# A Silu in a gated delta rule, queued on ScalarE behind the latest exponential of the keys' norms

## The chip, the cores and the metric

The kernel runs on one core of a Trainium2 chip. The metric is the device time of one execution, in microseconds (us); the runs shown are three, with their median and their ends. The profile is of one further execution, and its times count from the first profiled instruction. Engines are named as the profile names them: PE is TensorE's matmuls, PEld its weight loads, ACT is ScalarE, DVE is VectorE, POOL is GpSimd, SP issues the weight transfers.

## The reference

Two layers over x of shape 1 x 256 x 2048 in float32. Layer 0 is differential attention and a gated MLP with a short convolution. Layer 1 is the gated delta rule, which the change touches, and again the MLP:

```
def gated_deltanet(h, w_in, conv_w, a_log, dt_bias, norm_g, w_out):
    proj = h @ w_in
    ...
    qkv = jax.nn.silu(causal_dwconv(qkv, conv_w))
    q, k, v = jnp.split(qkv, [GDN_KEY_DIM, 2 * GDN_KEY_DIM], axis=-1)
    q = l2_norm(q.reshape(b_sz, s_len, GDN_QK_HEADS, GDN_HEAD_DIM).astype(jnp.float32))
    k = l2_norm(k.reshape(b_sz, s_len, GDN_QK_HEADS, GDN_HEAD_DIM).astype(jnp.float32))
    ...
    o = gated_delta_rule(q, k, v, g, beta)
    o = rms_norm(o, norm_g) * jax.nn.silu(z.reshape(b_sz, s_len, GDN_V_HEADS, GDN_HEAD_DIM).astype(jnp.float32))
    return o.reshape(b_sz, s_len, GDN_VALUE_DIM).astype(h.dtype) @ w_out

def l2_norm(x):
    return x * lax.rsqrt(jnp.sum(x * x, axis=-1, keepdims=True) + RMS_EPS)
```

There are 16 query and key heads of 128 and 32 value heads. So between the projection and the delta rule stand a four-tap convolution, a Silu, and for queries and keys a division by the root of a sum of squares. Inside the delta rule, decays are exponentials of differences of accumulated gates.

## The kernel before

**Dense products.** `dense` (L132) multiplies a weight block of 2048 x 256 by the 256 tokens. It goes through the 2048 rows in four chunks of four 128-row tiles. For each chunk `weights` (L81) transfers a 512 KB tile `raw` on the SP queue (L86), rounds it on ACT to the tile `whi` (the cast on L89) and takes the remainder on DVE as `wlo` (L90). PE then multiplies with both parts (L151, L152, and L154 where the product isn't `wide`). `raw`, `whi` and `wlo` have four buffers each. After every chunk `dense` calls `tick` (L71), which advances each background generator by one `yield`.

**The delta rule.** `gdn` (L542) works in four blocks of four head pairs. In each block the plan is: `("k", 0)` to `("k", 3)`, then `("v", 0)`, two z products, `("v", 1)` to `("v", 3)`, and the output product of the block before. For each `k` and `v` step, `lin` (L576) runs one dense product and scales it, and `convs` (L589) applies the four taps (`conv`, L301: one ACT instruction on L306 and three on DVE, L310, for each half) and then one Silu over 128 x 512 elements on ACT (L593). That is 32 Silus of this kind.

**A key pair's norms.** After each `k` step a generator `keys` (L596) is spawned. At its first advance it squares the Silu's output on ACT (L599) and splits the square into a high part (ACT, L321) and a low part (DVE, L322); `lows` keeps the latter. It then lets three advances pass. At the fourth, which is the last chunk of the next dense product, it emits the sums of squares on PE (L329, two matmuls over the two parts), the addition of the mask on DVE (L626), and then, under `lnexp` (L295), a load of ACT's table set that holds Ln and Exp (L297), the root as Ln (L316) and Exp (L317), and four exponentials of the decays (L631). `lnexp` puts these only behind its own table load, by `issue_after`. DVE then divides by the root (L632), and two advances later PE multiplies the normalised keys and queries (L639, L640) and DVE scales the products (L645, L647). In block 0 the first pair's generator waits until `lows` has two entries, so the roots of the first two pairs are both emitted in the third dense product.

**The order on an engine.** The kernel is built by a framework that keeps one queue for each engine and chooses the order in each queue at build time, from a simulated timeline and the order in which the program emits the instructions (`schedule_with_timeline_sim=True`). An instruction that isn't ready in that simulation can be overtaken by one emitted later. `with tc.issue_after(i)` adds an edge for the ordering alone: what the block emits on the engine of `i` is queued behind `i`. On the chip each engine works through its queue in order and waits by semaphores only for what it needs of other engines.

**Table sets.** Silu isn't in the set with Ln and Exp. Where an activation finds the other set active, the build puts an ACT_TABLE_LOAD in front of it, which the profile shows under the line of that activation: L593 for a Silu of `convs`, L317 and L631 for exponentials, L854 for the Silu of z. The loads on L297 are written in the program and are always there.

Of the kernel before, what the change touches and what calls it, by code (L numbers as in the profile page):

```python
# [10 lines left out]
AF = mybir.ActivationFunctionType  # L11
# [15 lines left out]
class Trunk:  # L27
# [37 lines left out]
    def mp(self):  # L65
        return self.mps.tile([P, 512], F32, tag="mp", name="mp")
# [246 lines left out]
    def rsqrt(self, out, ps, n):  # L313

        nc = self.nc
        nc.scalar.activation(out, ps, AF.Ln, bias=self.eps, scale=1.0 / n)  # L316
        nc.scalar.activation(out, out, AF.Exp, scale=-0.5)  # L317

    def split(self, out, a):

# [221 lines left out]
    def gdn(self, w_gate, w_in, w_z, w_out, nb, hb, gate_ap, const_ap, conv_col, ng, done):  # L542
# [7 lines left out]
        nc, tc, mp = self.nc, self.tc, self.mp  # L550
# [4 lines left out]
        with tc.tile_pool(name="gd", bufs=1) as gd:  # L555
# [15 lines left out]
            flat = "p i c -> p (i c)"  # L571
            nl = 4 * hb
            half = gd.tile([P, 2], F32, tag="half", name="half")
            gates, lows = {}, []

            def lin(w, wide):  # L576
                ps = self.dense(w, KD, self.h_acts, wide=wide)
                u = gd.tile([P, 2, T], F32, tag="u", name="u", bufs=1)
                if wide:
                    main, small = self.halves(ps)  # L580
                    uv = u.rearrange("p c (q j) -> p c q j", q=2)
                    nc.scalar.copy(uv, small)
                    nc.vector.tensor_tensor(uv, main, uv, ALU.add)
                    self.scale(u)
                else:
                    self.merge(ps, u)
                return u

            def convs(u, tiles):  # L589
                c = gd.tile([P, 2, T], F32, tag="cv", name="cv", bufs=4)  # L590
                for i in range(2):
                    self.conv(c[:, i, :], u[:, i, :], [conv_col(t, tiles[i]) for t in range(4)], None)
                nc.scalar.activation(c, c, AF.Silu)  # L593
                return c

            def keys(hq, c, cc, b0, res):  # L596

                sq = gd.tile([P, 2, T], F32, tag="qs", name="qs", bufs=2)
                nc.scalar.square(sq, c)  # L599
                sp = gd.tile([P, 2, 2, T], F32R, tag="qp", name="qp", bufs=1)  # L600
                lows.append(self.split(sp, sq))

                def fetch():
                    d = gd.tile([P, 2, 384], F32, tag="lt", name="lt", bufs=hb)
                    nc.sync.dma_start(d, gates["rows"][2 * hq:2 * hq + 2, :].unsqueeze(0).to_broadcast([P, 2, 384]))
                    return d

                d = fetch() if "rows" in gates else None
                for _ in range(3):
                    yield  # L610
                while "rows" not in gates:
                    yield
                if d is None:
                    d = fetch()
                    yield
                    yield
                    yield
                gc = gates["col"]
                dv = d[:, :, :T].rearrange("p v (t c) -> p v t c", t=2)
                m4 = mask.unsqueeze(1).unsqueeze(1).to_broadcast([P, 2, 2, P])  # L620
                pn = mp()
                sums = self.total(pn, [sp])
                while len(lows) < 2:
                    yield
                with tc.issue_after(lows[max(hq, 1)].ins):
                    nc.vector.tensor_tensor(dv, dv, m4, ALU.add)  # L626
                with self.lnexp(sums):
                    self.rsqrt(sq, self.apart(pn), 1)
                    for v in range(2):
                        for t, s in ((1, d[:, v, :P]), (0, d[:, v, P:])):  # L630
                            nc.scalar.activation(s, s, AF.Exp, bias=gc[:, t, 2 * hq + v:2 * hq + v + 1])  # L631
                nc.vector.tensor_tensor(c, c, sq, ALU.mult)  # L632
                q, k = c[:, 0, :], c[:, 1, :]
                yield
                yield
                prods = []
                for r in (k, q):
                    p = mp()
                    nc.tensor.matmul(p[:, :P], k[:, P:], r[:, P:], start=True, stop=True)  # L639
                    nc.tensor.matmul(p[:, P:384], k[:, :P], r, start=True, stop=True)  # L640
                    prods.append(p)
                lt = d
                qkt = gd.tile([P, 2, 384], F32, tag="qkt", name="qkt", bufs=hb)
                for v in range(2):
                    nc.vector.scalar_tensor_tensor(  # L645
                        qkt[:, v], prods[1][:, :384], P ** -0.5, d[:, v], ALU.mult, ALU.mult)
                    nc.vector.tensor_tensor(lt[:, v], prods[0][:, :384], d[:, v], ALU.mult)  # L647
                for v in range(2):
                    b = b0 + v
                    lv = lt[:, v, :T].rearrange("p (t c) -> p t c", t=2)  # L650
                    for r in quad:
                        nc.gpsimd.tensor_copy(
                            cc[r, :, 2 * b:2 * b + 2].rearrange("p c t -> p t c"), lv[r, :, r])
                    res.append((lt[:, v], qkt[:, v]))
# [180 lines left out]
            for b in range(nb):  # L835
# [5 lines left out]
                for op, i in plan + [("v", i) for i in range(1, hb)]:  # L841
                    if op == "k":
                        hq = heads[i]
                        c = convs(lin(w_in[hq * 2], 0 < b < nb - 1), (hq, nq + hq))
                        self.spawn(keys(hq, c, cc, 2 * i, lqs))
                        if i == hb - 1:
                            self.spawn(invert(b, cc, lqs, inv))
                            self.spawn(levels(lqs, inv, range(len(groups)), solved))
                    elif op == "z":
                        gr = groups[i]  # L850
                        zt = zts[i] = gd.tile([P, 2, gv, P], F32, tag="vz", name="zt", bufs=4)
                        ps = self.dense_tok(w_z[heads[gr[0]] // 2], KD, self.h_acts)
                        for t in range(2):
                            nc.scalar.activation(zt[:, t].rearrange(flat), ps[:, t, :], AF.Silu,  # L854
                                                 scale=self.rstdc[:, t:t + 1])
                    else:
                        gi = i // gh
                        gr = groups[gi]
                        if i == gr[0]:
                            vt = gd.tile([P, 2, gv, P], F32, tag="vz", name="vt", bufs=4)  # L860
                            ready = []
                            self.spawn(group(gi, gr, lqs, solved, vt, ready, zts, acts))
                        hq = heads[i]
                        c = convs(lin(w_in[hq * 2 + 1], True),
                                  (2 * nq + 2 * hq, 2 * nq + 2 * hq + 1))
                        self.spawn(to_tokens(c, vt, 2 * (i - gr[0]), ready))
# [216 lines left out]
```

## Time and profile before

| what | value |
|---|---|
| median of three runs | 2531.76 us (2530.8 to 2531.91) |
| profiled execution, span | 2530.1 us |
| median less span | 1.66 us |
| ACT busy | 1513.2 us, 60% of the span |
| DVE busy | 1908.3 us, 75% |
| ACT_TABLE_LOADs on L297 / L593 | 28 / 18 |
| key stages of blocks 0 to 3, about | 1095 to 1145, 1236 to 1300, 1434 to 1500, 1627 to 1690 us |

The span is from the first to the last profiled instruction, so what is measured outside it (1.66 us) is start and end. Busy shares are of the whole span. In the timeline each row has the start in us, the length in us, the engine, the line, the operation, the tiles it writes and reads, their shapes, and a count where equal neighbours are merged; a bracket at the end tells how long the engine was idle before it and what ended that. PE's rows have modelled ends, so its starts are what to compare.

### The profile page before, as it was taken

To read this page: it belongs to the slowest core of one execution; us is meant where nothing else is said; L and a number is where in the kernel's file an instruction comes from. 1 tells how busy PE (TensorE), PEld (TensorE's weight loads), DVE (VectorE), ACT (ScalarE), POOL (GpSimd) and SP (SyncE) were. 2 spreads that over 40 slices of the span, in tenths; PEclk is the share of its full clock that TensorE was granted. 3 is DMA by queue.
4 is the path that set the end of the run, shared out by engine and by line. 5 is a ranking of instruction groups with operands and counts; after the bars stand their busy time and mean duration, and the time that the engine had idled before them with its cause. 6 is when DMAs were issued, how large, how long until landed. Compare 5 with 4: busy or idle time off the path is not lost.

```text
span 2530.1 us, 41598 instructions
## 1 busy us (share of the span) xinstructions
PE 2520.0 (100%) x16151; PEld 2309.7 (91%) x16151; DVE 1908.3 (75%) x2847; ACT 1513.2 (60%) x2098; POOL 103.5 (4%) x197
## 2 busy tenths in 40 slices
PE   9999999999999999999999999999999999999999
PEld 8998899999999999998989989989999999999998
DVE  8886677777777555689788788788887777776544
ACT  7766656666666444485774675675566666665343
POOL 0000000000000000012021021021000000000000
PEclk9999999999999999999999999999999999999999
DMA  7555566666666666666455565555566666666775
GB/s 256 175 184 175 167 203 201 202 202 201 200 201 202 200 200 202 202 187 201 154 185 180 170 188 184 168 175 184 165 201 201 201 201 202 201 201 205 209 207 157
DMA packets 138199, 487.20 MB, mean 193 GB/s; under 512 B 15472, under 2 KB 18448, under 8 KB 138000
## 3 DMA queue, kind: packets, MB, share of 16 engines
q1 hardware_dynamic: 137712, 484.17, 60.8%
q8 instruction: 127, 2.08, 0.3%
q14 instruction: 72, 0.59, 0.1%
q10 hardware_dynamic: 288, 0.35, 0.0%
HBM read 482.32 MB, written 2.15 MB: 191 GB/s over the span
## 4 chain that ended last, share of the span: by engine, by line
PE 95%; ACT 3%; DVE 1%; issue 1%; DMA 0%; SPq 0%; ACTq 0%; DVEq 0%
PE ps L151 51%; PE ps L152 26%; PE ps L221 3%; PE ps L220 3%; PE ps L222 3%; PE mp L773 2%; PE mp L151 1%; PE ps L154 1%; ACT whi L89 1%; PE mp L329 1%; PE mp L152 0%; ACT L593 0%; ACT lt L631 0%; PE ps L123 0%; ACT L297 0%
## 5 line engine op out<-in xcount | busy, mean ns | idle before, releaser
L90 DVE TENSOR_TENSOR wlo<-raw,whi 128x1024 fp32r<-128x1024 f32 (+2 forms) x911 | 1104.1, 1213 | 506.1 <-ACT whi L89 498.2
L89 ACT CAST whi<-raw 128x1024 fp32r<-128x1024 f32 (+2 forms) x911 | 944.2, 1038 | 822.9 <-PE ps L151 657.0
L151 PE MATMUL ps<-h,whi 128*128 128x512 f32 (+1 forms) x4208 | 1369.4, 375 | 0.0
L152 PE MATMUL ps<-h,wlo 128*128 128x256 f32 x4208 | 1151.1, 274 | 1.0 <-DVE wlo L90 1.0
L151 PEld LDWEIGHTS ps<-h,whi 128*128 128x128 f32 x4208 | 796.1, 189 | 102.8
L152 PEld LDWEIGHTS ps<-h,wlo 128*128 128x128 f32 x4208 | 807.7, 192 | 2.8 <-DVE wlo L90 1.3
L151 PE MATMUL ps<-ac,whi 128*128 128x512 f32 x1546 | 506.8, 382 | 0.0
L152 PE MATMUL ps<-ac,wlo 128*128 128x256 f32 x1546 | 421.2, 273 | 0.0
L151 PEld LDWEIGHTS ps<-ac,whi 128*128 128x128 f32 x1546 | 292.1, 189 | 40.8 <-PE ps L151 0.2
L152 PEld LDWEIGHTS ps<-ac,wlo 128*128 128x128 f32 x1546 | 296.8, 192 | 0.1
L151 PE MATMUL ps<-oc,whi 128*128 128x512 f32 x512 | 170.7, 384 | 0.0
L220 PE MATMUL ps<-whi,h 128*128 128x512 f32 x384 | 146.5, 382 | 0.0
L221 PE MATMUL ps<-wlo,h 128*128 128x512 f32 x384 | 146.1, 380 | 0.0
L222 PE MATMUL ps<-whi,h 128*128 128x512 f32 x384 | 145.7, 379 | 0.0
L310 DVE SCALAR_TENSOR_TENSOR cv<-u,fcols,cv 128x255 f32<-128x255 f32 (+1 forms) x344 | 142.9, 477 | 0.0
L152 PE MATMUL ps<-oc,wlo 128*128 128x256 f32 x512 | 142.0, 277 | 0.0
L151 PEld LDWEIGHTS ps<-oc,whi 128*128 128x128 f32 x512 | 96.9, 189 | 12.5
L152 PEld LDWEIGHTS ps<-oc,wlo 128*128 128x128 f32 x512 | 98.3, 192 | 0.5
L308 ACT ACTIVATE cv<-u,fcols 128x256 f32<-128x256 f32 x172 | 93.9, 593 | 0.5 <-DVE u L205 0.5
L343 DVE TENSOR_TENSOR x<-ps,x 128x512 f32<-128x512 f32 x110 | 75.6, 687 | 12.5 <-PE ps L152 11.2
L310 DVE SCALAR_TENSOR_TENSOR cv<-u,cols,cv 128x255 f32<-128x255 f32 (+2 forms) x192 | 84.0, 486 | 0.3
L221 PEld LDWEIGHTS ps<-wlo,h 128*128 128x128 f32 x384 | 72.6, 189 | 10.0 <-DVE wlo L90 0.2
(220 smaller groups left out, 2077.3 us busy)
## 6 DMA issues: line engine op xcount, KB each, us to landing
raw<-w_up SPq DMA_DIRECT2D x344, 512.0 KB, 4.7
raw<-w_down SPq DMA_DIRECT2D x160, 512.0 KB, 3.8
raw<-w_in SPq DMA_DIRECT2D x128, 512.0 KB, 4.7
raw<-w_z SPq DMA_DIRECT2D x64, 512.0 KB, 3.7
raw<-w_out SPq DMA_DIRECT2D x64, 512.0 KB, 4.2
raw<-w_qk SPq DMA_DIRECT2D x56, 512.0 KB, 4.5
raw<-w_v SPq DMA_DIRECT2D x32, 512.0 KB, 3.5
raw<-w_o SPq DMA_DIRECT2D x32, 512.0 KB, 4.7
```

Of the source, the lines that this page charges most:

```text
L89: self.cast = nc.scalar.copy(hi[:, :, s], raw[:, :, s])
L90: nc.vector.tensor_tensor(lo[:, :, s], raw[:, :, s], hi[:, :, s].bitcast(F32), ALU.subtract)
L151: nc.tensor.matmul(bank[c][:, :n], hi[:, k, s], self.turns(a[:, :n // T, :]), start=first, stop=False)
L152: nc.tensor.matmul(bank[c][:, :T], lo[:, k, s], self.turns(a[:, :1, :]), start=False, stop=last and wide)
L154: nc.tensor.matmul(bank[c][:, :T], hi[:, k, s], self.turns(a[:, 1:, :]), start=False, stop=last)
L220: nc.tensor.matmul(ps[:, c, :], ah, wh, start=first, stop=False)
L221: nc.tensor.matmul(ps[:, c, :], ah, wl, start=False, stop=False)
L222: nc.tensor.matmul(ps[:, c, :], al, wh, start=False, stop=last)
L308: nc.scalar.activation(out, u, AF.Identity, bias=bias, scale=taps[n - 1])
L310: nc.vector.scalar_tensor_tensor(out[:, j:], u[:, :T - j], taps[n - 1 - j], out[:, j:], ALU.mult, ALU.add)
L343: self.nc.vector.tensor_tensor(x, part, x, ALU.add)
L773: nc.tensor.matmul(p[:, v, :], l(v), r[:, v, :], start=i == 0, stop=i == len(terms) - 1)
```

## The change

`rsqrt` (L313) now returns its exponential. `keys` appends that instruction to a list `roots`. In `convs`, if the list has an entry, the Silu is emitted inside `issue_after` of the latest one. The edge is on ACT alone and adds no semaphore. `rsqrt`'s other callers ignore the value. Of the 32 Silus, the first two of block 0 are emitted while the list is empty.

```
@@ rsqrt
         nc.scalar.activation(out, ps, AF.Ln, bias=self.eps, scale=1.0 / n)
-        nc.scalar.activation(out, out, AF.Exp, scale=-0.5)
+        return nc.scalar.activation(out, out, AF.Exp, scale=-0.5)
@@ gdn
-            gates, lows = {}, []
+            gates, lows, roots = {}, [], []
@@ convs
-                nc.scalar.activation(c, c, AF.Silu)
+                if roots:
+                    with tc.issue_after(roots[-1].ins):
+                        nc.scalar.activation(c, c, AF.Silu)
+                else:
+                    nc.scalar.activation(c, c, AF.Silu)
                 return c
@@ keys
                 with self.lnexp(sums):
-                    self.rsqrt(sq, self.apart(pn), 1)
+                    roots.append(self.rsqrt(sq, self.apart(pn), 1))
```

## The prediction

> **What bounds the kernel now.** I read the page first, then busy time by window over the four key stages of the delta rule, then the timeline of ACT, DVE and PE in the stretches where PE stands idle.
>
> ```profile
> span 2530.1 us, 41598 instructions
> PE 2520.0 (100%) x16151; PEld 2309.7 (91%) x16151; DVE 1908.3 (75%) x2847; ACT 1513.2 (60%) x2098; POOL 103.5 (4%) x197
> ```
>
> PE is busy 2520.0 of 2530.1 us. The change adds and removes no matmul, so all that it can give through PE's visible idle time is some of 10.1 us in the whole kernel. The windows tell how much of that lies in the key stages. Their columns are the length, then busy time with counts for PE, PEld, DVE, ACT and POOL, then clock, DMA share and GB/s.
>
> ```profile
> 1095.00:1145.00 50.00, 49.05 (x297) 44.70 (x296) 40.52 (x62) 44.12 (x66) 13.85 (x26) 1.00 0.62 193
> 1236.00:1300.00 64.00, 62.09 (x361) 56.00 (x360) 54.98 (x93) 58.96 (x86) 13.97 (x24) 1.00 0.50 153
> 1434.00:1500.00 66.00, 65.51 (x362) 58.84 (x362) 55.37 (x82) 58.97 (x85) 14.29 (x28) 1.00 0.58 177
> 1627.00:1690.00 63.00, 62.73 (x426) 58.02 (x426) 49.80 (x75) 53.85 (x77) 11.14 (x24) 1.00 0.53 160
> ```
>
> One row is one block. PE is idle 0.95 us in block 0 (50.00 less 49.05), 1.91 in block 1, 0.49 in block 2 and 0.27 in block 3: 3.62 us in all. ACT is busy 88%, 92%, 89% and 85% of them, far over its 60% of the span. Here, and only here, ACT is near enough to being the bound that its order can reach PE.
>
> **Which Silus move.** A pair's root is emitted in the last chunk of the next dense product, just ahead of that product's own Silu; in block 0 two roots come in the third product. So the edge names, for the Silus of pairs 1, 2, 3 and of the first values in each block (in block 0 from pair 2 on), an exponential that is only just emitted; for every other Silu it names one long done, and binds nothing. Where the queue already has that exponential first, nothing changes. Where it is overtaken, the exponential finds the Silu's table set active and needs a load of its own, so the overtakings can be counted in table loads. The first row below is of the view by source line (shortest, median and longest in ns, first and last start); the others are groups of ACT by line.
>
> ```profile
> L317 ACT ACT_TABLE_LOAD  x4: 1283/1283/1283, 1124.2 to 1491.1; - x4
> ```
>
> ```profile
> L631 ACT ACT_TABLE_LOAD x1 | 1.3, 1283 | 0.0
> L854 ACT ACT_TABLE_LOAD x1 | 1.3, 1283 | 0.0
> ```
>
> The four on L317 belong, in the timeline of ACT, to block 0 pair 3, block 1 pairs 1 and 2, and the first values of block 2. The one on L631 belongs to block 0 pair 2, and the one on L854 follows the overtaking in block 2, where the late exponential left the wrong set for z's Silu. So five Silus move, in blocks 0, 1 and 2, and none in block 3. With the exponential first, each place needs one load for its Silu and none to come back, since the load on L297 is written in the program anyway. Six loads of 1.283 us fall away: 7.70 us of ACT, 1513.2 to 1505.5. The loads on L593 and L297 stay at 18 and 28.
>
> **Block 1**, the largest term. ACT, then DVE, then PE:
>
> ```profile
> 1263.07 1.48 ACT L631 ACTIVATE lt<-lt,gc 128x128 f32<-128x128 f32 x4
> 1264.57 1.28 ACT L593 ACT_TABLE_LOAD   x1
> 1265.86 0.63 ACT L593 ACTIVATE cv<-cv 128x512 f32<-128x512 f32 x1
> ...
> 1267.44 1.28 ACT L317 ACT_TABLE_LOAD   x1
> 1268.74 0.63 ACT L317 ACTIVATE qs<-qs 128x512 f32<-128x512 f32 x1
> ```
>
> ```profile
> 1269.40 0.69 DVE L632 TENSOR_TENSOR cv<-cv,qs 128x512 f32<-128x512 f32 x1 [0.71 <-ACT qs L317]
> ```
>
> ```profile
> 1270.14 0.49 PE L639 MATMUL mp<-cv 128*128 128x128 f32 x2 [1.41 <-DVE cv L632]
> ...
> 1273.97 0.45 PE L329 MATMUL mp<-qp,onesr 128*128 128x512 f32 x1 [0.50 <-ACT whi L89]
> ```
>
> The exponential at 1268.74 stands behind a load, the Silu and a second load (3.19 us) and one cast. DVE's division waits for it, and PE's product of keys waits 1.41 us for DVE. With the order turned, both loads and the Silu leave from in front: the exponential starts at 1268.74 - 3.19 = 1265.55, the division ends 3.19 us sooner, and PE, which would have started at 1270.14 - 1.41 = 1268.73, finds it done at 1266.90. So the 1.41 us go. What is late next is the wait of 0.50 us at the sums: its input is ACT work queued behind this place, which comes 1.28 us sooner (one load less), against a PE that comes 1.41 us sooner. It stays at about 0.5. The nearest row of the order to come, and of what then is left, is block 2, whose second pair has its exponential first already:
>
> ```profile
> 1461.09 0.64 ACT L317 ACTIVATE qs<-qs 128x512 f32<-128x512 f32 x1
> ...
> 1463.98 0.63 ACT L593 ACTIVATE cv<-cv 128x512 f32<-128x512 f32 x1
> ```
>
> ```profile
> 1467.12 0.48 PE L329 MATMUL mp<-qp,onesr 128*128 128x512 f32 x1 [0.49 <-ACT qp L321]
> ```
>
> There PE waits 0.49 us at the sums and nowhere else in the stage. I take block 1's idle time to fall from 1.91 to between 0.27 and 0.50: a gain of 1.4 to 1.6.
>
> **Block 0.** ACT, then DVE, then PE:
>
> ```profile
> 1102.61 0.63 ACT L593 ACTIVATE cv<-cv 128x512 f32<-128x512 f32 x1
> ...
> 1104.08 0.63 ACT L599 ACTIVATE qs<-cv 128x512 f32<-128x512 f32 x1
> 1104.73 1.28 ACT L631 ACT_TABLE_LOAD   x1
> 1106.03 1.49 ACT L631 ACTIVATE lt<-lt,gc 128x128 f32<-128x128 f32 x4
> ...
> 1110.80 0.61 ACT L321 CAST qp<-qs 128x512 fp32r<-128x512 f32 x1
> 1111.31 1.05 ACT L89 CAST whi<-raw 128x1024 fp32r<-128x1024 f32 x1
> 1112.26 0.63 ACT L317 ACTIVATE qs<-qs 128x512 f32<-128x512 f32 x1
> ```
>
> ```profile
> 1104.65 0.69 DVE L626 TENSOR_TENSOR lt<-lt,con 128x512 f32<-128x512 f32 x1 [2.02 <-DMA lt<-grow]
> ...
> 1111.45 0.69 DVE L322 TENSOR_TENSOR qp<-qs,qp 128x512 fp32r<-128x512 f32 x1 [1.56 <-ACT qp L321]
> ```
>
> ```profile
> 1113.93 0.38 PE L152 MATMUL ps<-h,wlo 128*128 128x256 f32 x1 [0.95 <-DVE wlo L90]
> ...
> 1117.12 0.57 PE L329 MATMUL mp<-qp,onesr 128*128 128x512 f32 x1
> ```
>
> Pair 2's Silu at 1102.61 must now stand behind the exponential at 1112.26. With it go its square and its cast of `qp`. The four decay exponentials at 1106.03 need the masked rows of DVE, ready at 1104.65 + 0.69 = 1105.34, so of what leaves from in front of them they gain only 0.69 us. The cast of `qp` at 1110.80 (0.61) goes too, so the weight cast at 1111.31 comes 0.69 + 0.61 = 1.3 us sooner, and DVE no longer waits 1.56 us for `qp` ahead of the remainder that PE lacks at 1113.93. That covers the 0.95 us. I book 0.7 to 0.95 of it, since pair 3's moved Silu and a later pair 2 may bring back a wait like block 2's.
>
> **Block 2** gains two loads (2.57 us of ACT), but its PE wait at 1467.12 lies before the overtaking; nothing to gain, 0. In front of z's products a Silu that comes one exponential later is covered by the casts that run ahead of PE. What is queued behind a moved Silu is its own square and the weight casts; the SP queue isn't touched, but a `raw` buffer comes free when its cast and remainder are done, so a shift of a cast shifts a transfer equally, at 50% to 62% DMA share.
>
> A rule speaks to the loads' price: on the row above, the Silu at 1265.86 starts 0.01 us after its load ends (1264.57 + 1.28), so a switch costs 1.28 us. The Trainium skill, page "ScalarE: Activation LUTs", section "What ACT_TABLE_LOAD costs", has the same 1283 ns and adds a drain of 1380 ns, 2.66 us for each switch; by that, ACT would be freed of 16.0 us instead of 7.7. The trace shows no such drain around the loads.
>
> **The sum.** 1.5 (block 1) + 0.6 (block 0: 0.8 booked, less about 0.2 for what comes back) = 2.1 us. The profiled execution would go from 2530.1 to 2528.0, and with the 1.66 us that the median lies above it, the time is 2529.7. The most that the visible idle time allows is all four windows, 3.62 us: 2528.1. A measurement of this kernel can tell about 0.2%, 5.1 us, from no change, so this is a forecast of no change by that bound.
>
> **Rivals.**
> - *The wait moves to the sums* (25%). Take block 0 with nothing ahead sooner: the exponential ends at 1112.89, then a load (1.28), the Silu (0.63), its square (0.63), the cast (0.61) and DVE's low part (0.69) end at 1116.73. PE wants its sums at 1117.12 - 0.95 = 1116.17: 0.56 us late. With the 1.3 us worked out above it is 0.7 early instead. Each weight cast queued between adds 1.05; with two on the late end it is 2.7 late, the gain of 0.95 is more than lost, and with block 1's 1.4 the time is 2531.76 - 1.4 - 0.95 + 2.7 = 2532.1. One cast gives 2531.0. Against it: the build's simulation orders PE as well, and can move the sums back behind other matmuls. For it: blocks 2 and 3 still wait a little there.
> - *Slower by over 0.2%* (5%). The same mechanism with PE's order unmoved and four casts between, 0.56 + 4.20 = 4.76 us, in block 0, and half of that, 2.4, at block 1's sums, which already wait; less block 1's 1.4: +5.8, 2537.5. It decides from the third cast on. Against it: in the block 2 rows 2.25 us lie from the exponential's end to the Silu, which is a load and one cast.
> - *PE is starved without showing idle* (6%). Weight loads are busy 92% of block 3 (58.02 of 63) but 89%, 88% and 89% of blocks 0, 1 and 2. Were PE's busy time partly hidden waiting, and all three rose to block 3's share, they would take 48.5, 60.8 and 63.9 us in place of 50, 64 and 66: 6.8 us less, 2525.0; with block 1 and 0 alone 4.7, 2527.1. The Trainium skill, page "Perfetto Trace Analysis", section "Identifying the Most-Contended Engine", holds that matmul busy time is a bad measure and weight-load busy share a good one. Against it: block 3 differs in its product's shape, and has other small matmuls in its window.
> - *It does not do what it says* (7%). The edge names the root's exponential and not the four decay exponentials; if the build's order puts a Silu between them, a load on L631 takes the place of one on L317, as the row at 1104.73 shows. ACT's time and PE's waits stay: 2531.8.
>
> **How the numbers follow.** The forecast has 57%. Its own range is 2528.1 to 2530.5. The range of 8 in 10 adds the moved wait (up to one further cast over its 2532.1: 2533.2) and at the low end the smaller case of hidden starvation with some tolerance: 2527.3 to 2533.2. Faster by over 0.2% (under 2526.7) is the larger half of the 6%: 0.04. Slower (over 2536.8) is 0.05. Same is 0.91.
>
> **What would show it.** Loads: L317 4 to 0, L631 and L854 1 to 0, L593 18, L297 28, ACT near 1505.5. In every key stage the order Ln, decays, Exp, load, Silu. PE idle in the windows of blocks 0 and 1 at 0.3 to 0.5, as in 2 and 3, and no wait of L639 on L632. Wrong would be: loads left on L317; a wait over 1 us at L329 in block 0 or 1; a time that moves by more than the 3.62 us of idle time, which would mean that PE's busy rows hide waiting.

## The result and the profile after

The changed kernel takes 2526.80 us (median of 18 runs, 2526.3 to 2527.79) against 2531.82 us for the kernel before (18 runs, 2530.57 to 2532.68): 5.0 us less, a ratio of 0.9982 with a 95% interval of 0.9975 to 0.9988. That is about the bound of 0.2% that the prediction named. It is more than twice the 2.1 us forecast, and 0.5 us below the range.

The page's first lines after, to set beside those of before:

```profile
span 2524.6 us, 41598 instructions
PE 2517.5 (100%) x16151; PEld 2309.3 (91%) x16151; DVE 1904.7 (75%) x2847; ACT 1505.3 (60%) x2092; POOL 100.3 (4%) x197
```

The same 16151 matmuls, and six fewer ACT instructions (2098 to 2092), which are the six table loads: ACT falls from 1513.2 to 1505.3 us, forecast 1505.5. The groups of ACT by line show the loads that are left (the Silu's two lines are now L595 with the edge and L597 without):

```profile
L297 ACT ACT_TABLE_LOAD x28 | 35.9, 1283 | 10.7 <-PE mp L329 8.5 <-PE mp L282 1.7
L595 ACT ACT_TABLE_LOAD x17 | 21.8, 1283 | 0.3
...
L597 ACT ACT_TABLE_LOAD x1 | 1.3, 1283 | 0.7 <-DVE cv L310 0.7
```

None stands on L317, on the decays or on z's Silu any more, and 17 + 1 remain for the Silus. What the change does to the moved Silus was read rightly. Pair 2 of block 1, in the timeline of ACT, has the forecast order of decays (now L635), exponential, load and Silu. But the taps and a weight cast now stand ahead of the exponential, and it starts at 1267.81, where the prediction had 1265.55:

```profile
1264.69 1.48 ACT L635 ACTIVATE lt<-lt,gc 128x128 f32<-128x128 f32 x4
1266.07 0.89 ACT L306 ACTIVATE cv<-u,cols 128x256 f32<-128x256 f32 x2
1266.87 1.03 ACT L89 CAST whi<-raw 128x1024 fp32r<-128x1024 f32 x1
1267.81 0.63 ACT L317 ACTIVATE qs<-qs 128x512 f32<-128x512 f32 x1
1268.45 1.28 ACT L595 ACT_TABLE_LOAD   x1
1269.75 0.63 ACT L595 ACTIVATE cv<-cv 128x512 f32<-128x512 f32 x1
```

Where PE gained is seen in busy time by window: the four key stages (taken a little wider than in the prediction, so that they hold the same stages in both kernels) and the last output product. Before:

```profile
1095.00:1150.00 55.00, 54.05 (x321) 49.08 (x320) 43.47 (x67) 47.85 (x70) 17.15 (x34) 1.00 0.62 193
1236.00:1304.00 68.00, 66.09 (x384) 59.55 (x383) 58.11 (x97) 60.92 (x90) 14.68 (x27) 1.00 0.52 162
1430.00:1503.00 73.00, 72.51 (x401) 65.16 (x400) 60.47 (x92) 63.36 (x88) 15.75 (x32) 1.00 0.57 177
1622.00:1692.00 70.00, 69.73 (x480) 64.78 (x479) 56.52 (x86) 57.41 (x82) 12.35 (x26) 1.00 0.55 170
1790.00:1880.00 90.00, 90.00 (x559) 82.99 (x558) 77.87 (x120) 57.20 (x86) 0.00 (x0) 1.00 0.59 191
```

After:

```profile
1095.00:1150.00 55.00, 55.00 (x326) 50.16 (x325) 43.87 (x67) 44.70 (x68) 11.79 (x28) 1.00 0.66 203
1236.00:1304.00 68.00, 68.00 (x393) 61.73 (x392) 56.38 (x92) 58.99 (x87) 11.65 (x24) 1.00 0.52 158
1430.00:1503.00 73.00, 73.00 (x401) 65.67 (x400) 61.20 (x90) 61.75 (x88) 15.63 (x31) 1.00 0.59 180
1622.00:1692.00 70.00, 70.00 (x465) 65.30 (x464) 58.58 (x88) 58.50 (x83) 16.35 (x32) 1.00 0.57 175
1790.00:1880.00 90.00, 89.31 (x554) 82.07 (x553) 77.81 (x120) 58.28 (x88) 0.00 (x0) 1.00 0.59 189
```

PE's idle time in the key stages goes from 0.95 + 1.91 + 0.49 + 0.27 = 3.62 us to nothing, in blocks 2 and 3 too, and 0.69 us of new idle time appears at the output product. That is 2.93 us of visible gain; the time fell by 5.0. The weight loads (PEld, the second busy time of a row) tell more: in the four key stages they rise from 238.57 to 242.86 us, by 4.3 us.

So idle time is too coarse here, and for what follows I use a finer measure. **Loss** is, summed over PE's matmuls in a window, the time from one matmul's start to the next's, less the median of that time over all matmuls of the same tiles and shape in the kernel before. Over the delta rule (1056 to 1875 us) it is 13.06 us before and 8.07 after: 4.99 less, as much as the medians differ by. (The two profiled executions differ by 5.5 us, 2530.1 to 2524.6. The rest, 0.4, lies ahead of the delta rule, where the code is the same and the loss still varies from 6.0 to 7.1 us over all kernels.) By window:

| kernel | block 0 | block 1 | block 2 | block 3 | last output |
|---|---|---|---|---|---|
| window, us | 1095-1150 | 1236-1304 | 1430-1503 | 1622-1692 | 1790-1880 |
| before | 1.27 | 2.44 | 0.79 | 1.51 | 0.13 |
| after | 0.05 | 0.00 | 0.02 | 0.23 | 1.09 |
| edge in block 0 | 0.29 | 1.26 | 0.78 | 1.54 | 0.14 |
| edge in block 1 | 1.51 | 0.02 | 0.78 | 1.49 | 0.14 |
| edge in block 1, pair 1 | 1.46 | 1.02 | 0.78 | 1.51 | 0.14 |
| edge in block 1, pair 2 | 1.71 | 0.94 | 0.78 | 1.51 | 0.13 |
| edge in block 2 | 1.65 | 2.43 | 0.79 | 1.56 | 0.13 |
| edge in blocks 0, 1 | 0.05 | 0.00 | 0.02 | 1.48 | 0.14 |
| edge in blocks 0, 1, values of 2 | 0.16 | 0.00 | 0.02 | 1.53 | 0.14 |
| edge in blocks 0, 1, 2 | 0.70 | 0.00 | 0.03 | 0.80 | 1.09 |
| order of before, no Silu loads | 0.35 | 0.01 | 0.02 | 0.16 | 0.14 |
| order of after, no Silu loads | 0.05 | 0.00 | 0.02 | 0.15 | 1.09 |
| loads put back | 0.28 | 0.34 | 0.05 | 0.23 | 12.39 |

Blocks 1 to 3 repeat to 0.1 us where the queues are the same. Block 0 doesn't: with its queue unchanged it shows 1.27 to 1.71, with the edge 0.05 to 0.70.

### The profile page after: what moved, and what is told of

Same layout as the page of the kernel before. It is cut to its first block, busy times and chain, and to the rows that moved or that the text cites. A ratio compares the mean times of both kernels' runs of the same rounds, so it can differ in the third digit from the quotient of the medians.

```text
span 2524.6 us, 41598 instructions
## 1 busy us (share of the span) xinstructions
PE 2517.5 (100%) x16151; PEld 2309.3 (91%) x16151; DVE 1904.7 (75%) x2847; ACT 1505.3 (60%) x2092; POOL 100.3 (4%) x197
## 4 chain that ended last, share of the span: by engine, by line
PE 99%; DMA 0%; SPq 0%; DVE 0%; ACT 0%; issue 0%; DVEq 0%
PE ps L151 53%; PE ps L152 27%; PE ps L220 3%; PE ps L221 3%; PE ps L222 3%; PE mp L777 2%; PE ps L154 1%; PE mp L151 1%; PE mp L329 1%; PE mp L644 1%; PE mp L152 0%; PE ps L123 0%; PE mp L742 0%; PE mp L760 0%; PE mp L643 0%; PE mp L822 0%
## 5 line engine op out<-in xcount | busy, mean ns | idle before, releaser
L220 PEld LDWEIGHTS ps<-whi,h 128*128 128x128 f32 x384 | 72.6, 189 | 10.0
```

The lines of the kernel that those rows point to most:

```text
L220: nc.tensor.matmul(ps[:, c, :], ah, wh, start=first, stop=False)
```

## The experiments

Eleven kernels were run, each against the kernel before in the same session. Most keep the edge for some of the Silus only. For these a list `now` holds the block, the kind of step and its number (the block alone, where only blocks are told apart):

```
             for b in range(nb):
                 ...
                 for op, i in plan + [("v", i) for i in range(1, hb)]:
+                    now[:] = b, op, i
...
-                if roots:
+                if roots and now[0] == 0:
                     with tc.issue_after(roots[-1].ins):
```

The condition is what differs from kernel to kernel. An edge in block 3 alone (`now[0] == 3`) was built and not run, since it gives the queues of the kernel before, instruction for instruction: as the prediction had counted, none of those Silus is overtaken there, and such an edge costs nothing.

**Edge in block 0 alone.** `now[0] == 0`.

> The edge is kept in block 0 of the delta rule alone, so two of the five moved Silus move. Theory A (each wait goes where its own Silu moves): PE's loss falls by about 1.2 us in block 0 and by nothing in blocks 1, 2 and 3: 2530.6 against 2531.8, with the waits of 1.41 us (keys' product, block 1) and 0.49 us (sums, block 2) still there. Theory B (a moved Silu changes the order that the build chooses for everything behind it, so waits go in blocks whose Silus stay): blocks 1 to 3 change too, by a us or more in sum, either way; 2529 or lower if they follow the changed kernel.

2529.33 us, against 2531.68; ratio 0.9990 (0.9982 to 0.9999). Block 0's loss falls by 0.98. Blocks 2 and 3 keep theirs, as theory A has it, but block 1, where no Silu has the edge, falls by 1.18. Its queue differs: the wait of 1.41 us at the keys' product is gone, and PE waits elsewhere in the stage instead, in front of a z product:

```profile
1286.82 0.48 PE L221 MATMUL ps<-wlo,h 128*128 128x512 f32 x1 [0.98 <-DVE wlo L90]
```

Neither theory is whole: an edge reaches into the next block, and there it can move a wait as well as take it. PE's own order is another there too: the keys' product that had waited stands 28 matmuls later than before, and the sums behind it 32.

**Edge in block 1 alone.** `now[0] == 1`.

> The edge is kept in block 1 alone (two moved Silus). Theory A: the loss of block 1 falls by 1.5 to 2.4 us, blocks 2 and 3 keep their waits at the sums: 2529.4 to 2530.3. Theory B: blocks 2 and 3, behind it, lose their waits as well (0.8 and 1.3 us in the changed kernel): 2527.5 to 2528.

2529.28 us, ratio 0.9989 (0.9980 to 0.9998). Block 1's loss goes to 0.02, by 2.42, and blocks 2 and 3 stay. That is theory A, at its upper end. PE's order hardly differs here (that keys' product stands 4 matmuls earlier, the sums 3), and DVE's division in front of that product ends at 1266.16 instead of 1270.09.

**Edge in block 2 alone.** `now[0] == 2`, which moves the Silu of the first values.

> The edge is kept in block 2 alone (one moved Silu, that of the first values, behind the wait of 0.49 us at the sums). Theory A: no gain, 2531.8, since no PE wait stands behind that place in block 2. Theory B: block 3's order is made anew and its loss of 1.5 us falls or rises; block 2's own wait ahead of the place stays at 0.49 us; 2530.5 if block 3 follows the changed kernel.

2531.54 us, ratio 0.9999 (0.9990 to 1.0008): nothing, in any block, as the prediction had it for this term.

**One Silu at a time in block 1.** `now == [1, "k", 1]` and `now == [1, "k", 2]`.

> The edge is kept for one Silu alone, that of pair 1 in block 1. In the built queues ACT's differs by this move and nothing else. No PE wait stands at that place. Theory A (each wait goes where its own Silu moves): nothing, 2531.7, and block 1 keeps its waits of 1.41 us at the keys' product and 0.50 us at the sums. Theory C (ACT and DVE are one unbroken chain from here to those waits, so a load taken out anywhere ahead comes off them): block 1's loss falls from 2.4 us by the 1.28 us of one load, to about 1.2: 2530.4.

> The edge is kept for one Silu alone, that of pair 2 in block 1, directly ahead of the wait of 1.41 us. Theory A, as the prediction put it: the 1.41 us go and the wait at the sums stays at 0.5 us or a little more, since ACT comes 1.28 us sooner and PE 1.41: loss 2.4 to 0.8, 2530.1. Theory C, with a chain that holds more: the sums' wait goes as well, loss near 0: 2529.3.

Both 2529.97 us against 2531.57, ratio 0.9994 (0.9985 to 1.0003 and 1.0002), which alone would not be clear of no change; the loss in block 1, which repeats to 0.1, is. It falls from 2.44 to 1.02 with pair 1's Silu and to 0.94 with pair 2's, by 1.42 and 1.50, and with both by 2.42. Pair 1's Silu stands 26 us and more ahead of the waits, and PE waits for nothing there. The move is a clean one: in the traces ACT's order differs from that of the kernel before in this one place, and the orders of DVE, PE and POOL do not differ at all. With that move alone the wait at the keys' product is gone, and the one at the sums is left. In PE's timeline with pair 1, then with pair 2:

```profile
1271.73 0.45 PE L329 MATMUL mp<-qp,onesr 128*128 128x512 f32 x1 [0.50 <-ACT whi L89]
```

```profile
1271.93 0.46 PE L329 MATMUL mp<-qp,onesr 128*128 128x512 f32 x1 [0.68 <-DVE oc L826]
```

So theory C holds: the load of 1.28 us, needed by the exponential that pair 1's Silu had overtaken, came off a wait 25 us later. The chain of waits of the kernel before shows the path that carries it, from that load on L317 without a break to the wait at the sums:

```profile
1244.81 1.28 ACT L317
1246.10 0.64 ACT qs L317
...
1254.92 1.13 DVE wlo L90
1256.06 0.93 DVE qkt L645 x2
...
1260.14 1.03 ACT whi L89
1261.18 1.28 ACT L297
...
1267.44 1.28 ACT L317
1268.74 0.63 ACT qs L317
...
1272.98 0.95 ACT whi L89
...
1273.97 0.45 PE mp L329
```

It goes through ACT, then DVE, then ACT. (What the view calls issue between these pieces, up to 1.1 us each, is time in which a row of the same engine still runs.) With pair 2 alone, the 1.41 us go and the sums wait 0.68 us, near the 0.5 that the prediction had for the whole block. That is in part luck, since PE has a few matmuls in another order here, and the sums start 2.04 us sooner. From this kernel to the edge in all of block 1, pair 1's Silu is again the only move, and the loss falls from 0.94 to 0.02.

**Edge in blocks 0 and 1.** `now[0] < 2`.

> The edge is kept in blocks 0 and 1 (four of the five moved Silus). In the built queues of ACT the difference to the kernel before reaches through block 2 and ends ahead of block 3. Theory A (each wait goes where its own Silu moves): blocks 0 and 1 lose 1.2 and 2.4 us of waiting, block 2 keeps its 0.8 and block 3 its 1.5: about 2528.2. Theory B (the order made anew behind a moved Silu takes the later waits away): block 2's 0.8 goes too, block 3 keeps its 1.5: about 2527.4.

2527.20 us, ratio 0.9983 (0.9974 to 0.9992). Block 2's loss goes from 0.79 to 0.02 although none of its Silus has the edge, and block 3 keeps 1.48: theory B, for block 2. It isn't the loads. In this kernel block 2 has more of them on L317, since other Silus now overtake; the view of L317 by line has

```profile
L317 ACT ACT_TABLE_LOAD  x3: 1283/1283/1283, 1448.0 to 1491.4; - x3
```

where the kernel before has one in this block. What differs is the order, and PE's own above all. The next two rows are PE's, from the start of the kernel up to these sums, for the kernel before and for this one; the count in brackets is the number of matmuls that PE has started ahead of them:

```profile
0.00:1467.11 1467.11, 1461.05 (x9244) 1.00 0.62 193
0.00:1467.44 1467.44, 1464.95 (x9274) 1.00 0.59 194
```

The build has put the sums behind 30 more matmuls. ACT's cast of `qp`, which they wait for, ends only 1.4 us sooner than before (1465.71 against 1467.07), while PE comes to the old place, behind 9244 matmuls, at 1462.33. There it would have waited 3.4 us. The wait goes because PE needs the sums later, and not because ACT has them sooner.

**Edge in blocks 0 and 1 and for the first values of block 2.** `(now[0] < 2 or now == [2, "v", 0])`, exactly the five Silus that were overtaken before.

> The edge is kept in blocks 0 and 1 and for the first values of block 2, which is all five moved Silus and nothing else; only the Silus of pairs in block 2 and all of block 3 are without it. If it is the moved Silus' loads, it is the changed kernel: 2526.8. If it is the order, which here joins that of the kernel before ahead of block 3, block 3 keeps its 1.5 us and the output product after it has no wait of 0.7 us: 2527.2.

2526.90 us, ratio 0.9982 (0.9973 to 0.9991). The loss is as the second reading expects: block 3 keeps 1.53 and the output product has no wait. The two differences to the changed kernel, 1.3 more and 0.95 less, leave it level with it in time.

**Edge in blocks 0, 1 and 2.** `now[0] < 3`.

> The edge is kept in blocks 0, 1 and 2, so none of block 3's Silus has it; before the change none of those is overtaken. The built queue differs from that of the changed kernel in a few rows of block 3 only. Theory A: the edges in block 3 do nothing, 2526.8, but block 3's loss should have stayed at 1.5 us in the changed kernel too, which it did not. Theory B: block 3's loss falls to about 0.2 us as in the changed kernel, through the order behind the five moved Silus: 2526.8; if it is the edges of block 3 that do it, the loss stays at 1.5 us: 2528.1.

2527.38 us, ratio 0.9983 (0.9974 to 0.9992). Block 3's loss is 0.80, halfway. Its view of L317 has loads in block 3, where the kernel before had none:

```profile
L317 ACT ACT_TABLE_LOAD  x2: 1283/1283/1283, 1639.1 to 1666.1; - x2
```

Behind the changed order of block 2, Silus of block 3 do overtake, and in the changed kernel block 3's own edges stop them. So of the 1.28 us that block 3 gained, about 0.7 came with the order from ahead and about 0.6 with its own edges. The expectation had only the two ends.

**The order of before, without the Silus' loads.** In the kernel before, Exp stands in place of the convolutions' Silu, so the results are others. Of the 55 table loads 39 are left; in the key stages those on L297 and, at the end of each, one for z's Silu.

```
-                nc.scalar.activation(c, c, AF.Silu)
+                nc.scalar.activation(c, c, AF.Exp)
```

> The kernel before with Exp in place of Silu in the convolutions (the delta rule's inputs are then exponentials, not Silus): the instructions stand in the same order on each engine, and no table load is needed between these and the roots, some 20 loads of 1.28 us fewer. Theory A and B both say that PE's waits in the key stages come of ACT being late by load time: they nearly all go, 4 to 5 us faster, about 2527 to 2528. Rival (the order itself costs, whatever the loads): the exponential that waits behind the Silu and a cast keeps most of its wait, and the time falls by 2 us or less.

2525.66 us, ratio 0.9976 (0.9967 to 0.9986). With each engine's order untouched, the loss of all four key stages goes to 0.54 in sum, from 6.01. So in that order PE's waits are ACT's lateness, and enough load time taken out cures all of them.

**The order of after, without the Silus' loads.** The same edit on the changed kernel, with the same 39 loads left.

> The changed kernel with Exp in place of Silu in the convolutions (the delta rule's inputs are then exponentials): its order on each engine, without the loads. If loads alone are the price and the order is not, it comes to the same time as the order of before without loads, 2525.7. If the order of the changed kernel has a cost of its own (a wait of 0.7 us at the output product at 1804 us), that stays: 2526.4 to 2526.7.

2526.59 us, ratio 0.9980 (0.9971 to 0.9989): 0.9 us slower than the order of before without these loads. The difference is the last output product, 1.09 against 0.14. The wait that the changed kernel shows there comes of its order and not of loads:

```profile
1804.60 0.48 PE L151 MATMUL ps<-oc,whi 128*128 128x512 f32 x1 [0.69 <-DVE oc L826]
```

**Loads put back.** In the changed kernel a further load of the exponentials' set stands between the exponential and the Silu.

```
                     with tc.issue_after(roots[-1].ins):
+                        p = nc.scalar.preload_act_table_set(LNEXP)
+                    with tc.issue_after(p.ins):
                         nc.scalar.activation(c, c, AF.Silu)
```

> The changed kernel with one more table load, 1.28 us, behind each exponential that a Silu is queued behind: 30 more loads, 16 of them in the key stages, four to a block. If ACT's time in the key stages is what PE waits for, PE's loss returns there by one to three us a block: 2530 to 2536. If only the order counts, the order stays nearly that of the changed kernel and so does the time: 2527 to 2528.

There are 72 loads instead of 49. 2550.64 us, ratio 1.0072 (1.0059 to 1.0085): 19 us slower than before, beyond both expectations, and not where they put it. The key stages lose under 0.4 us each; 12.1 and 12.4 us are lost in 1304 to 1430 and 1790 to 1880 us. The longest of PE's waits are

```profile
PE ps L151 <- ACT zt L860: 4.8, 1, 4.8
PE mp L645 <- DVE cv L638: 2.4, 1, 2.4
```

The further instruction also made the order on every engine anew, so this gives no price of a load; it shows only what an unlucky order can cost.

## Why the prediction was wrong

**Which Silus move, and the loads: right.** Five Silus, six loads, L317 and the others to zero, 7.9 us of ACT against 7.70, and no gain from the moved Silu in block 2.

**The step that failed: the order of everything but the moved Silus was taken as given.** The build chooses it anew behind the first edge. For block 1 the prediction had a division that ends "3.19 us sooner", at 1266.90, ahead of a PE that keeps its order. In the changed kernel the division ends at 1270.86, which is 0.8 us later than before. PE doesn't wait, because the keys' product now stands behind 41 more matmuls and starts at 1274.61, where it was 1270.14 before. DVE, then PE:

```profile
1270.18 0.68 DVE L636 TENSOR_TENSOR cv<-cv,qs 128x512 f32<-128x512 f32 x1
```

```profile
1274.40 0.38 PE L221 MATMUL ps<-wlo,h 128*128 128x512 f32 x1
1274.61 0.39 PE L643 MATMUL mp<-cv 128*128 128x128 f32 x2
```

The sums of blocks 1, 2 and 3 that waited before stand 35, 30 and 24 matmuls later. PE's rows up to them, three of before and three of after, with the count of matmuls in brackets:

```profile
0.00:1273.96 1273.96, 1268.39 (x7907) 1.00 0.62 195
0.00:1467.11 1467.11, 1461.05 (x9244) 1.00 0.62 193
0.00:1658.85 1658.85, 1652.72 (x10695) 1.00 0.61 192
0.00:1276.99 1276.99, 1274.19 (x7942) 1.00 0.63 196
0.00:1467.50 1467.50, 1464.70 (x9274) 1.00 0.62 194
0.00:1657.09 1657.09, 1654.29 (x10719) 1.00 0.62 193
```

At their old places PE would have come 5.0, 3.4 and 2.3 us ahead of the cast that they need: after the change its matmuls of those numbers start at 1269.97, 1462.39 and 1653.36, and the casts of `qp` end at 1274.94, 1465.77 and 1655.67. The prediction had named this, as an argument against its first rival (the build "can move the sums back behind other matmuls"), but gave it no term.

**Block 1 was mis-sized: 1.5 booked, 2.4 gained.** By the prediction's own mechanism, too, its term was too small: the edge in block 1 alone, with PE's order nearly that of before, gains 2.42. The wrong step there is that the wait at the sums "stays at about 0.5", because ACT came "1.28 us sooner (one load less)". Two loads leave this block. Pair 1's was left out, since PE has no wait where it stands, but it is on the same unbroken chain as the later waits, and taken out alone it gains 1.42. The chain of waits, read over the whole stage instead of the last 10 us, shows it. Either way no wait is left, so the gain is the same; that the changed kernel gains in block 1 what the loads alone would gain is luck.

**Block 0 was mis-sized: 0.6 booked, about 1.3 gained.** The mechanism was right: the remainder that PE lacked is ready at 1111.09 after the change, and PE comes to it at 1112.37. The gain is the mean of the five kernels without the edge there, 1.52, less that of the five with it, 0.25; single pairs differ by 0.6 to 1.7. Part of it is that idle time understates a wait:

```profile
1111.94 0.38 PE L151 MATMUL ps<-h,whi 128*128 128x512 f32 x1
1112.16 0.27 PE L152 MATMUL ps<-h,wlo 128*128 128x256 f32 x1
...
1112.59 0.38 PE L151 MATMUL ps<-h,whi 128*128 128x512 f32 x1
1113.93 0.38 PE L152 MATMUL ps<-h,wlo 128*128 128x256 f32 x1 [0.95 <-DVE wlo L90]
```

The matmul with 0.95 us of idle time ahead started 1.335 us after the one before it, where 0.218 is usual, so the wait cost 1.12. The 0.2 taken off for a wait that comes back shows in one run alone, the edge in blocks 0, 1 and 2, where block 0's sums wait 0.38 us.

**Blocks 2 and 3: 0 booked, 0.8 and 1.3 gained.** The prediction had "nothing to gain, 0" for block 2 and no term for block 3. The edge in blocks 0 and 1 clears block 2 with no edge and more loads in it, and in block 3 about half came with the order. The same remaking cost 0.96 us at the last output product. Taking block 2 as the row "of the order to come" for block 1 was therefore a bad model: its wait, too, came and went with one order.

**The bound of 3.62 us of visible idle time did not hold.** The prediction said that a larger change "would mean that PE's busy rows hide waiting", and they do: a row of 0.38 us with 0.22 us to the next start covers 0.16 us of any wait. The rival of hidden starvation, held at 6%, had this mechanism right for part of the gain; it would have put block 1 at a weight-load share of 92%, and 61.73 of 68 us is 91%. The page "Perfetto Trace Analysis" of the Trainium skill, section "Identifying the Most-Contended Engine", tells to judge PE by weight loads and not by matmul busy time. In these windows the trace agrees in direction: the weight loads show 4.3 us more where the matmul rows show 3.6 us less of idle time, and the loss falls by 5.7.

Of the rivals, the wait moved to the sums did not come in the changed kernel, nor did the slower case. In sum over the delta rule: 1.22 + 2.44 + 0.77 + 1.28 less 0.96, and 0.2 in the stretches between, make the 5.0.

What stays open is why the order behind the edges comes out better in block 3 and worse at the output product. The runs show that it is the order, not by which rule of the build. Nor is it shown how the changed kernel's gain in block 1 would be shared between the loads and the order. No version ran clearly faster than the changed kernel: in the order of before and without the Silus' loads, which isn't the same computation, it is 1.1 us less.

## What to carry to other kernels

A wait is paid from anywhere on the unbroken chain that ends in it: follow the chain of waits back to its last real pause, and count every instruction removed along it, also where the waiting engine lost nothing. Where a build orders the queues, an edge for one instruction changes the order behind it; compare the built queues, that of the waiting engine too, and expect waits behind it to come and go by a us. A wait that is gone does not show that its input came sooner: look at when the input was ready, and at how much other work the engine now does ahead of it. The idle time of a pipelined engine understates its waits: measure from start to start, or by the work done in a window.

## What the runs showed of the hardware

A table load costs its 1.283 us each time it is in the queue, also where the set is active already: after the change the root of block 0's second pair is loaded behind exponentials of the same set, in ACT's timeline.

```profile
1104.02 1.50 ACT L635 ACTIVATE lt<-lt,gc 128x128 f32<-128x128 f32 x4 [1.50 <-DVE lt L630]
1105.54 1.28 ACT L297 ACT_TABLE_LOAD   x1
1106.83 0.69 ACT L316 ACTIVATE qs<-mp,eps 128x512 f32<-128x512 f32 x1
```

Nothing else was unexpected. Extra time around a switch, which the prediction had looked for, showed in no run: in every kernel ACT's next instruction starts 0.01 us after the end of a load (median).
